# Placing every split weight load 60 places earlier in the scheduling order of a two-layer hybrid decoder trunk

## The chip, the cores and the metric

The kernel is one program on one core of a Trainium2 chip. The metric is the device time of one execution in microseconds (us), as the median of several runs. Beside it stands one execution that was taken with the hardware profiler; its span is the time from the first to the last instruction that the profiler recorded.

## The reference

Two layers act on a sequence of 512 tokens with 1024 features, in 32-bit floats. What one layer computes, cut to what matters here:

```
h = rmsnorm(x, norm_mix_pre)
proj = h @ w_in
q, k, v, rw, gate_a, gate_b = _split(proj, ...)
y_att = sliding_window_attention(rope(q), rope(k), v, att_sinks) @ w_o_att
y_rw = rwkv7_time_mix(rw, ...) @ w_o_rw          # delta-rule state over the tokens
mixed = sigmoid(gate_a) * y_att + sigmoid(gate_b) * y_rw
x = x + rmsnorm(mixed @ w_out, norm_mix_post)
u = causal_dwconv(rmsnorm(x, norm_ffn_pre) @ w_up, conv_w, conv_b)
ua, ub = _split(u, (FFN_DIM, FFN_DIM))           # FFN_DIM = 2816
x = x + rmsnorm((gelu(ua) * ub) @ w_down, norm_ffn_post)
x = x + rmsnorm(sigmoid(x @ w_ple_gate) * (p[i] @ w_ple), norm_ple)
```

## The kernel before

All activations are held with features on the 128 partitions and the 512 tokens along the free axis, so a weight matrix is cut into tiles of 128 x 128 and one output tile is 128 features by 512 tokens. `KT` is 8: a product over 1024 features has 8 such k-tiles, the product over the 2816 features of `w_down` has 22.

**A product in three parts.** Each operand is split into a high part, rounded to the fast matmul format `F32R`, and a low part, the rest. `mm3` (L250 to L252) adds three matmuls for each k-tile: high weight by high activation, high weight by low activation, low weight by high activation.

**A weight load.** `load_w` (L134) brings up to four k-tiles at once, 256 KB: a DMA into `w`, which SyncE issues (L122); on ScalarE the rounding copy into `wh` (L125); on VectorE the difference `w` minus `wh` into `wl` (L155). The buffers come in two classes. Class `m` has two buffers for `w` and three each for `wh` and `wl`, class `f` has one for `w` and two each for the others. Most loops take the classes in turn; inside the attention and state stages most loads are of class `m`. `proj` issues, for each four k-tiles, one load and the twelve matmuls that use it. So a load with its matmuls takes 15 places in program order, a product over eight k-tiles 30 places, one output tile of `w_down` 84.

A second group of helpers, `raw_w`, `split_raw` and `keep_w`, loads weights which are kept for later; their raw DMA target comes from the same `w` buffers when no other pool is named, but the code is not `load_w`.

**The stages of a layer**, in program order: a lead-in that normalizes and computes a few small projections; attention (`w_q`, `w_g`, `w_ga`); four groups of the state stage (`rwkv_group`), in each of which `rwkv_prep` runs twice and projects with `w_k`, `w_wa2`, `w_r` and `w_v`, `rwkv_inverse` makes a triangular inverse of 62 dependent VectorE steps and several small DMAs, and then eight chunks are scanned one after another with small matmuls; the gate `w_gb`; the output products `w_oa` and `w_or`; `w_out`; a small product with `w_ple`, whose results are stored as `ed`; the convolution stage (`ffn`, 44 products with `w_up`, each followed by one rescaling `un`, one ScalarE and two VectorE steps `cv`); `w_down`, with four `keep_w` loads of `w_pg` put between its columns; and the gate `w_pg`.

**What sets the order.** The program is written in one sequence, and each instruction's priority is its place in that sequence. A scheduler of the tile framework then builds the queue of each engine before the program runs: among the instructions that it takes to be ready, the one with the lowest number goes first. The queues are then fixed, and the engines work through them in order, with semaphore waits where an operand or a buffer is not free. A block under `tc.high_priority(offset=n)` gives the instructions in it numbers that are `n` lower. The seams between the stages use an offset of 3000 (`turn`), and `behind` and `issue_after` tie some instructions behind a named one. Before the change, the products of the convolution stage stood under an offset of 40, loads and matmuls together.

## Time and profile before

| what | us |
| --- | --- |
| median of 3 runs | 2319.58 |
| lowest and highest | 2317.64 and 2322.39 |
| the profiled execution | 2329.03 |
| its span | 2327.3 |
| mean granted TensorE clock in it | 0.981 of full speed |

In the profile, TensorE's matmuls stand as PE, its weight loads into the array as PEld, VectorE as DVE, ScalarE as ACT, GpSimd as POOL and SyncE's queue as SP or SPq. A group is a line of the kernel with its engine, operation and tiles; after the bar come busy time, the mean of one instruction in ns, and the idle time of that engine just before, with what ended it. A wait is written as the engine and tile that waited, the work that released it, the total in us, how often, and the longest. A helper's line stands for all its callers, so L125 and L122 are told apart by the tile names. One caution holds throughout: matmuls overlap in the hardware and their ends are modelled, so the mean of one 128x512 matmul in the records is longer than the distance between two starts.

### The profile page before, as it was taken

What the parts mean: (1) busy time and instruction counts of PE and PEld (TensorE: products, weight loads), DVE (VectorE), ACT (ScalarE), POOL (GpSimd) and SP (SyncE); (2) the same over time, 40 slices, a digit from 0 to 9 for tenths busy, and PEclk for the clock granted to TensorE, in tenths of its full rate; (3) what the DMA queues carried; (4) which work ended last, traced back from release to release, by engine and by line L of the source; (5) the groups of instructions that cost most, each with busy time, mean ns of one, the idle gap of its engine ahead of it and who ended that gap; (6) DMA issues with size and microseconds to landing.
All of it is one profiled execution on the core that took longest, in us unless ns stands there. A gap on an engine that the chain in (4) does not pass through costs nothing. (4 is left out here: it accounts for less than half of the span.)

```text
span 2327.3 us, 39473 instructions
## 1 busy us (share of the span) xinstructions
PE 2228.8 (96%) x14340; PEld 1740.2 (75%) x14340; DVE 1546.9 (66%) x3683; ACT 1109.6 (48%) x2450; POOL 27.1 (1%) x86
## 2 busy tenths in 40 slices
PE   7999999999999999999899999998999999999997
PEld 6766776667689777788896677766777887777886
DVE  6764678767566777743877647778656667776346
ACT  5566455544444544432445655545443544444332
POOL 1000000000000000000000000000000000000000
PEclk9999999889999999999999999999999999999998
DMA  4532332245571423233234333333356623223432
GB/s 150 168 94 97 99 94 79 75 121 171 176 259 31 128 91 98 89 118 116 86 124 148 98 104 98 83 92 103 113 159 212 213 78 92 95 95 90 126 98 69
DMA packets 204515, 269.40 MB, mean 116 GB/s; under 512 B 71840, under 2 KB 84640, under 8 KB 204320
## 3 DMA queue, kind: packets, MB, share of 16 engines
q1 hardware_dynamic: 204320, 266.88, 37.3%
q8 instruction: 113, 1.85, 0.3%
q14 instruction: 82, 0.67, 0.1%
HBM read 218.95 MB, written 42.47 MB: 112 GB/s over the span
## 5 line engine op out<-in xcount | busy, mean ns | idle before, releaser
L155 DVE TENSOR_TENSOR wl<-w,wh 128x512 fp32r<-128x512 f32 (+2 forms) x574 | 373.9, 662 | 317.4 <-ACT wh L125 292.7
L125 ACT ACTIVATE wh<-w 128x512 fp32r<-128x512 f32 (+1 forms) x590 | 348.8, 604 | 477.8 <-PE pm L251 134.7
L250 PE MATMUL pm<-hh,wh 128*128 128x512 f32 x1040 | 423.0, 412 | 4.6 <-ACT wh L125 2.4
L252 PE MATMUL pm<-hh,wl 128*128 128x512 f32 x1040 | 417.1, 408 | 7.4 <-DVE wl L155 7.2
L251 PE MATMUL pm<-hl,wh 128*128 128x512 f32 x1040 | 416.3, 404 | 0.0
L250 PEld LDWEIGHTS pm<-hh,wh 128*128 128x128 f32 x1040 | 196.8, 189 | 63.3 <-ACT wh L125 11.2
L252 PEld LDWEIGHTS pm<-hh,wl 128*128 128x128 f32 x1040 | 196.9, 189 | 57.5 <-DVE wl L155 13.6
L251 PEld LDWEIGHTS pm<-hl,wh 128*128 128x128 f32 x1040 | 197.4, 190 | 44.1 <-issue 7.2
L250 PE MATMUL pf<-hh,wh 128*128 128x512 f32 x512 | 208.3, 407 | 9.5 <-ACT hh L125 3.6
L251 PE MATMUL pf<-hl,wh 128*128 128x512 f32 x512 | 203.7, 398 | 0.0
L252 PE MATMUL pf<-hh,wl 128*128 128x512 f32 x512 | 203.5, 398 | 0.1
L134 DVE SCALAR_TENSOR_TENSOR cv<-un,vec,cv 128x511 f32<-128x511 f32 (+1 forms) x176 | 130.5, 749 | 40.6 <-ACT cv L125 38.1
L250 PEld LDWEIGHTS pf<-hh,wh 128*128 128x128 f32 x512 | 96.2, 188 | 42.7 <-ACT wh L125 8.5
L252 PEld LDWEIGHTS pf<-hh,wl 128*128 128x128 f32 x512 | 96.6, 189 | 27.0 <-issue 4.4
L251 PEld LDWEIGHTS pf<-hl,wh 128*128 128x128 f32 x512 | 96.7, 189 | 19.6 <-issue 1.8
L125 ACT ACTIVATE cv<-un,vec 128x512 f32<-128x512 f32 x88 | 71.1, 814 | 66.7 <-DVE un L128 66.7
L250 PE MATMUL pm<-uh,wh 128*128 128x512 f32 (+1 forms) x248 | 89.2, 360 | 3.5 <-ACT wh L125 3.4
L252 PE MATMUL pm<-uh,wl 128*128 128x512 f32 (+1 forms) x248 | 89.3, 360 | 0.0
L251 PE MATMUL pm<-ul,wh 128*128 128x512 f32 (+1 forms) x248 | 88.9, 359 | 0.0
L128 DVE TENSOR_TENSOR acc<-acc,sq 128x256 f32<-128x256 f32 (+1 forms) x114 | 50.0, 463 | 31.2 <-ACT sq L125 30.5
L533 DVE CUSTOM_DVE_ANT_0 sm<-scores,tmask 128x256 f32<-128x256 f32 (+1 forms) x128 | 43.5, 385 | 37.3 <-PE scores L117 37.1
L697 DVE TENSOR_TENSOR Z<-rin,Z 128x126 f32<-128x126 f32 (+22 forms) x248 | 62.3, 251 | 4.3
(409 smaller groups left out, 4468.9 us busy)
## 6 DMA issues: line engine op xcount, KB each, us to landing
w<-in_w_up_dram SPq DMA_DIRECT2D x156, 256.0 KB
w<-in_w_dn_dram SPq DMA_DIRECT2D x80, 256.0 KB
w<-in_w_q_dram SPq DMA_DIRECT2D x32, 256.0 KB
w<-in_w_ga_dram SPq DMA_DIRECT2D x32, 256.0 KB
w<-in_w_k_dram SPq DMA_DIRECT2D x32, 256.0 KB
w<-in_w_r_dram SPq DMA_DIRECT2D x32, 256.0 KB
w<-in_w_v_dram SPq DMA_DIRECT2D x32, 256.0 KB
w<-in_w_gb_dram SPq DMA_DIRECT2D x32, 256.0 KB
```

The costliest lines, as they stand in the source:

```text
L125: return self.nc.scalar.activation(out=out, in_=in_, func=func, **kw)
L128: return self.nc.vector.tensor_tensor(out=out, in0=in0, in1=in1, op=op)
L134: return self.nc.vector.scalar_tensor_tensor(out=out, in0=in0, scalar=s, in1=in1, op0=op0, op1=op1)
L155: self.nc.vector.tensor_tensor(out=wl, in0=w, in1=wh.bitcast(F32), op=ALU.subtract)
L250: mm(ps, wh, ah, start=start, stop=False)
L251: mm(ps, wh, al, start=False, stop=False)
L252: return mm(ps, wl, ah, start=False, stop=stop).ins
L533: nc.vector.tensor_tensor_reduce(out=sm[i][:, par * 256:par * 256 + KW], in0=scs[par][:, x * 256:x * 256 + KW], in1=tm, scale=1.0, scalar= ...
L697: nc.vector.tensor_tensor(out=tv, in0=rin[:, jj:jj + 1, jj + 1:].broadcast_to([P, n, nt]), in1=zt[:, :n, jj:jj + 1].broadcast_to([P, n, nt ...
```

## The change

`load_w` keeps the choice of the buffer class and then puts everything else, the DMA, `wh`, the optional partial corrections (L148) and `wl`, under an offset of 60. The body moves to a new method without another edit. In the convolution stage, the block with the offset of 40 goes away: its matmuls return to their own places, and its loads go from 40 to 60 places ahead.

```diff
@@ -139,6 +139,10 @@
             self.nw = (self.nw + 1) % 2
             cls = "mf"[self.nw]
         nb = {"m": (2, 3, 3), "f": (1, 2, 2)}[cls]
+        with self.tc.high_priority(offset=60):
+            return self.load_parts(src, kn, width, cls, nb, low)
+
+    def load_parts(self, src, kn, width, cls, nb, low):
         w = self.wpool.tile([P, kn, width], F32, name="w", tag="w" + cls, bufs=nb[0])
         self.dma(w, src)
         wh = self.wpool.tile([P, kn, width], F32R, name="wh", tag="wh" + cls, bufs=nb[1])
@@ -1098,8 +1102,7 @@
                 for k, w in enumerate(ahead[m]):
                     self.mm3(ps, w, h[k], k == 0, k == KT - 1)
             else:
-                with self.tc.high_priority(offset=40):
-                    ps = self.proj(a["w_up"][l, m], h, key=m)
+                ps = self.proj(a["w_up"][l, m], h, key=m)
             t, s = Y("cv"), F("un")
             self.tt(s, ps, self.rs, ALU.mult)
             self.act(t, s, AF.Identity, scale=vv("cw2")[:, m:m + 1], bias=vv("cb")[:, m:m + 1])
```

No instruction, transfer or buffer is added or removed. The loads that `raw_w` and `keep_w` make keep their places.

## The prediction

> **What bounds the kernel now.** I read the page first, then the stretches of 50 us, then TensorE's own waits.

> ```profile
> span 2327.3 us, 39473 instructions
> PE 2228.8 (96%) x14340; PEld 1740.2 (75%) x14340; DVE 1546.9 (66%) x3683; ACT 1109.6 (48%) x2450; POOL 27.1 (1%) x86
> L155 DVE TENSOR_TENSOR wl<-w,wh 128x512 fp32r<-128x512 f32 (+2 forms) x574 | 373.9, 662 | 317.4 <-ACT wh L125 292.7
> L125 ACT ACTIVATE wh<-w 128x512 fp32r<-128x512 f32 (+1 forms) x590 | 348.8, 604 | 477.8 <-PE pm L251 134.7
> ```

> TensorE is busy 2228.8 of 2327.3 us, so all its idle time together is 98.5 us. The change can take away idle time of TensorE and nothing else: the two split operations cost 662 and 604 ns before and after, 574 and 590 times. The idle time is spread unevenly.

> ```profile
> 350.00:400.00 50.00, 44.66 (x405) 29.28 (x404) 46.28 (x131) 29.05 (x69) 1.75 (x5) 0.98 0.31 87
> 400.00:450.00 50.00, 49.64 (x569) 33.81 (x569) 29.52 (x85) 24.62 (x70) 0.00 (x0) 0.78 0.26 76
> 850.00:900.00 50.00, 50.00 (x216) 39.57 (x215) 36.40 (x55) 23.01 (x36) 0.00 (x0) 1.00 0.29 95
> ```

> The columns are the stretch, its length, then busy time of PE, PEld, DVE, ACT and POOL, the granted clock, the DMA share and GB/s. In the convolution stage (850 to 900) TensorE has no idle time at all. In the state stage (350 to 400) it is idle for 5.34 us and VectorE is busy for 46.28 of 50. The list of TensorE's waits names what ends them:

> ```profile
> PE lead L250 <- ACT kwh L125: 15.3, 1, 15.3
> PE rstd L290 <- DVE nry L134: 8.3, 6, 6.5
> PE pm L252 <- DVE wl L155: 8.0, 10, 1.7
> PE pm L250 <- ACT wh L125: 7.4, 8, 1.9
> PE pm L250 <- ACT yr L125: 5.8, 4, 2.2
> PE A L117 <- DVE AR L128: 5.3, 3, 2.4
> PE half L250 <- ACT tg L125: 5.0, 1, 5.0
> PE pf L250 <- ACT hh L125: 3.6, 2, 2.4
> PE pm L600 <- ACT thw L125: 2.9, 2, 2.0
> PE A L117 <- DVE AM L128: 2.7, 4, 1.9
> PE pf L250 <- ACT wh L125: 2.5, 5, 0.8
> PE ple L250 <- ACT wh L125: 2.1, 2, 1.0
> PE pf L252 <- DVE wl L155: 0.4, 1, 0.4
> ```

> The first row is the start of the kernel, loaded through `raw_w`, which the change doesn't touch. The rows that end in `wh` or `wl` are those a load can cause: 8.0 + 0.4 for `wl` and 7.4 + 2.5 + 2.1 for `wh`, **20.4 us in all**, 0.9% of the span. The rest waits for other results.

> **The change part by part.** *Work.* Nothing is added or removed, so every engine's own sum is the same, zero us. Each load moves with its DMA issue on SyncE, its `wh` on ScalarE and its `wl` on VectorE, 60 places, which is two products of 30 places. How far it can really move is set by the buffers: class `m` holds three `wh`, class `f` two, so at most five loads, two and a half products, can stand ahead of the matmuls. The page's row of `wh` shows 134.7 us of ScalarE idle until a matmul (L251) gives a `wh` buffer back. Those loads are already as early as their buffers let them be, and a smaller number moves none of them. So only the others count.

> *The waits for wl, 8.4 us.* One of the longest, with the VectorE rows before it:

> ```profile
> 387.75 0.68 DVE L128 TENSOR_TENSOR Di<-k,Di 128x512 f32<-128x512 f32 x1
> 388.35 0.19 DVE L699 TENSOR_TENSOR Z<-Z 128x45 f32<-128x45 f32 x1
> 388.47 0.68 DVE L155 TENSOR_TENSOR wl<-w,wh 128x512 fp32r<-128x512 f32 x1
> 389.20 0.50 PE L252 MATMUL pm<-hh,wl 128*128 128x512 f32 x1 [1.37 <-DVE wl L155]
> ```

> `wl` stands in a busy queue behind steps of the same preparation (`Di`) and of the inverse (`Z`), and TensorE waits 1.37 us for it. `Di` stands less than 60 places ahead of the products it overlaps, so the new number lets `wl` pass it; one place earlier in the queue is worth 0.68 us here, two cover the whole wait. Bounds: 0 and 8.4 us. I take all **8.4**, because the cause here is queue order on VectorE, just what the change acts on.

> *The waits for wh, 12.0 us.* Here the transfer is late. An example, in SyncE's and ScalarE's queues:

> ```profile
> 394.08 0.33 SPq L122 DMA_DIRECT2D yrd<-yo  x1
> 394.45 0.92 SPq L122 DMA_DIRECT2D w<-in_w_v_dram  x2
> 398.14 0.63 ACT L125 ACTIVATE wh<-w 128x512 fp32r<-128x512 f32 x1 [2.54 <-DMA w<-in_w_v_dram]
> 397.26 1.16 PE L117 MATMUL A<-AR,bk 64*128 64x128 f32 x16 [2.38 <-DVE AR L128]
> ```

> The two `w_v` loads are issued right behind a store of the group before; the first lands for 398.14. A load whose issue passes such a store gains what the store holds up. TensorE's 2.38 us before the `A` matmuls is put down to `AR`, but with `w_v` in place it would have had other matmuls to run. A further case is the small `w_ple` product, whose loads share SyncE with the `ed` stores, and the columns of `w_down`. There, the chain that ended last runs through the one buffer of class `f`:

> ```profile
> 2158.50 2.65 DMA w<-in_w_pg_dram
> 2161.17 0.64 ACT kwh L125
> 2161.83 0.70 DVE kwl L128
> 2162.55 2.71 DMA w<-in_w_dn_dram
> ```

> A `w_pg` load of `keep_w`, which keeps its place, holds that buffer from 2158.50 to 2162.55, 4.05 us. The `w_down` loads, 60 places earlier, may now pass it. But a landing that is late because its buffer was late stays late. Bounds: 0 and 12.0; nothing tells the two kinds apart row by row, so I take half, **6.0**.

> *What is pushed back.* Each load that moves forward puts something else back by one `wl` or `wh`, 0.66 or 0.60 us. This costs only where TensorE already waits for such a result: `yr` 4 times, `AR` 3, `hh` 2, `thw` 2, `AM` 4, 15 waits in the rows above. With 0.66 us each that is 9.9 us; the other end is nothing. `AR`, `AM` and `thw` stand in the preparation, where the loads are passed over them, so 9 of the 15, **6.0 us**, is my value.

> *The matmuls of the convolution stage* lose their 40 places. In that stage TensorE's queue holds no other work than these products, and the row at 850 shows it full, so their order among themselves stays; 0. At its front the products of `w_ple` come first again, by program order; each matmul has to be run once in either order. If that cover failed, the stage would show idle time that it doesn't have now. Its loads go from 40 to 60 places, bounded by the same five buffers; 0. A later `un` can hold back an accumulator, but three accumulators give it two further products to finish in; 0.

> *The sum*: 8.4 + 6.0 - 6.0 = 8.4 us off the profiled span, 2327.3 to 2318.9. The profiled execution took 2329.03, of which 1.7 lie outside the span, and stands 9.45 above the median. I take the same 8.4 off the median: 2319.58 - 8.4 = **2311.2 us**, 0.36% faster.

> *The clock.* The stretch from 400 to 450 has the clock at 0.78, with TensorE busy for 49.64 us of it, many of them tiny matmuls. 22% of 50 us, 11 us, is the most that a better filled stretch there could give; it stays out of the sum, because I can't tell whether the loads would fill it. [...]

> **The rivals.**

> *Buffers, not places: no change.* The 134.7 us above, 105 times, is ScalarE waiting for TensorE. If the 20.4 us are likewise set by buffers and landings, gains and push-backs cancel: 2319.6, with 3 us to either side. Against it stands the `wl` case, which is a matter of places in one queue.

> *A load parks in front of the scan: slower.* ScalarE and VectorE work through fixed queues. A `wh` that was put ahead of a scan step's copy (`scr`, `X`, `Y`), because the scheduler took its transfer as landed, stalls that copy until the transfer has really landed. The place is the `w_k` load that opens each preparation while the group before is scanned:

> ```profile
> ACT wh L125 <- DMA w<-in_w_k_dram: 35.2, 10, 7.4
> PE xs L778 <- ACT scr L125: 2.0, 4, 0.8
> ```

> ScalarE already waits 35.2 us there in 10 waits, at no cost now, as the scan's own wait for `scr` is just 2.0 us. If each of the ten came ahead of a scan step and TensorE had nothing else, the price would be 35.2 us: 2354.8. With other products covering half, 17.6 us: 2337.2. It decides as soon as more than 8.4 of these 35.2 us fall on the scan. For it: 60 places reach back over the 39 closing steps of a group and into its last chunk, which has 34. Against it: the other seven chunks are out of reach. [...]

> *More than the sum*: all 20.4 us, the 5.3 us of `AR` and the 11 us of clock, 36.7 us in all: 2282.9.

> *The change does nothing it says* is excluded only in part: the numbers do change, but a queue that is already in this order stays so. It is the first rival's case.

> **How the numbers follow.** The forecast, 4.6 to 15 us faster, 0.48; more than that, 0.08; no change, 0.23; slower, 0.21. About 0.2%, 4.6 us, is what a measurement of this kernel can tell from no change. So faster 0.56, same 0.23, slower 0.21. The range goes from 2288, where nothing is pushed back and the clock is won as well (2319.6 - 20.4 - 11 = 2288.2), to 2335, just under the half price of the slower rival; each side leaves out about one in ten. Gains alone: 2304 to 2315.

> **What would show it.** Right: the two `wl` rows among TensorE's waits fall from 8.4 to under 3 us, the three `wh` rows from 12.0 to about 6, the `AR`, `AM` and `thw` rows grow by up to 6 us, and TensorE's idle sum falls from 98.5 to about 90. The convolution stretches stay at 50.00. Wrong, to the slow side: new rows of TensorE waiting on `scr`, `X` or `Y`, or idle time in the convolution stage; the clock in the state stage under 0.9 in more stretches than now. Wrong, to the other: state stage and `w_down` shorter by more than their waits.

## The result and the profile after

| | before | after |
| --- | --- | --- |
| median us (4 runs each) | 2319.93 | 2280.27 |
| lowest and highest | 2317.64, 2322.39 | 2275.79, 2284.78 |
| span of the profiled execution | 2327.3 | 2274.1 |
| mean granted clock in it | 0.981 | 0.993 |

The ratio is 0.9825, with a 95% interval from 0.9807 to 0.9843: **39.7 us faster**. The forecast was 8.4 us, and the time lies below its range. Of the four runs after, three list a mean clock of 0.990 to 0.993 and one, of 2284.78 us, lists 0.942; no trace of that run is kept, so this figure stays unexplained.

The page of the kernel after, and its stretches of 50 us beside those quoted of before (stretch, length, busy PE, PEld, DVE, ACT and POOL with the count of instructions, granted clock, DMA share, GB/s):

```profile
span 2274.1 us, 39486 instructions
PE 2192.8 (96%) x14340; PEld 1730.1 (76%) x14340; DVE 1544.7 (68%) x3683; ACT 1120.0 (49%) x2450; POOL 26.7 (1%) x86
```

```profile
350.00:400.00 50.00, 48.74 (x440) 33.47 (x435) 47.21 (x134) 29.05 (x71) 1.75 (x5) 1.00 0.32 90
400.00:450.00 50.00, 47.87 (x618) 32.36 (x618) 37.75 (x102) 29.62 (x82) 0.53 (x1) 1.00 0.31 86
850.00:900.00 50.00, 50.00 (x222) 41.42 (x221) 37.85 (x55) 24.61 (x37) 0.00 (x0) 1.00 0.32 95
```

TensorE's own busy time fell by 36.0 us, from 2228.8 to 2192.8, with the same 14340 matmuls; its idle time fell only from 98.5 to 81.3. So most of the gain lies where TensorE counted as busy. Two columns show it. From 400 to 450 the clock went from 0.78 to 1.00. From 850 to 900, where busy was 50.00 and still is, the *count* went from 216 to 222.

The waits that the prediction worked with, in the kernel after:

```profile
PE pm L254 <- ACT wh L125: 6.0, 9, 1.3
PE A L117 <- DVE AM L128: 4.1, 9, 1.8
PE pm L604 <- ACT thw L125: 3.7, 4, 1.8
PE pm L256 <- DVE wl L159: 2.9, 5, 0.9
PE A L117 <- DVE AR L128: 1.2, 1, 1.2
PE pf L254 <- ACT wh L125: 0.6, 2, 0.3
```

The rows that end in `wl` or `wh` went from 20.4 to 9.5 us.

Two parts of the program hold most of the gain. The first two rows are the state stage's scans of each layer, from their first small matmul (`xs`) to the first product of `w_or`; the last two are the convolution stage of each layer, from the last `w_ple` matmul to the first of `w_down`. Before:

```profile
337.10:625.30 288.20, 277.53 (x2685) 196.13 (x2682) 205.59 (x561) 141.98 (x355) 4.73 (x14) 0.93 0.40 117
1492.10:1773.40 281.30, 268.88 (x2684) 191.35 (x2683) 206.69 (x561) 142.07 (x354) 4.73 (x14) 0.97 0.41 121
766.50:987.40 220.90, 218.72 (x938) 173.21 (x937) 165.02 (x246) 105.54 (x164) 0.00 (x0) 1.00 0.31 96
1912.60:2134.20 221.60, 220.41 (x939) 170.53 (x938) 165.40 (x246) 104.72 (x163) 0.00 (x0) 1.00 0.31 97
```

After:

```profile
337.70:605.20 267.50, 261.82 (x2683) 183.62 (x2682) 202.54 (x559) 140.83 (x353) 4.72 (x14) 1.00 0.42 125
1458.30:1730.00 271.70, 262.45 (x2684) 183.91 (x2682) 203.66 (x559) 140.48 (x354) 4.72 (x14) 1.00 0.42 123
745.30:959.70 214.40, 212.99 (x938) 175.63 (x937) 169.56 (x250) 112.53 (x169) 0.00 (x0) 1.00 0.33 101
1869.00:2083.40 214.40, 212.93 (x938) 175.65 (x937) 169.16 (x250) 112.50 (x168) 0.00 (x0) 1.00 0.34 102
```

The scans take 569.5 us before and 539.2 after, 30.3 less; the convolution stages 442.5 and 428.8, 13.7 less; the rest of the 53.2 us between these two spans is 9.2.

Multiply length by mean clock in the scan rows: 268.0 and 272.9 before, 267.5 and 271.7 after. The clock has two digits, so each product is good to about 1.4 us; within that, both kernels need the same time at full clock. **Nearly the whole gain in the scans is clock**: before, 7% and 3% of the two stretches, 20.2 and 8.4 us, were lost to half clock. This is an account of the time, not yet a cause: TensorE's idle time in the same rows fell too, from 23.1 to 14.9 us. Where one such spell of before begins and ends (windows of a few us, same columns):

```profile
390.00:397.00 7.00, 4.80 (x20) 3.30 (x18) 6.19 (x14) 1.75 (x3) 1.22 (x4) 1.00 0.64 156
397.00:400.00 3.00, 2.33 (x20) 1.52 (x20) 2.41 (x5) 1.26 (x2) 0.00 (x0) 0.73 0.72 150
400.00:421.00 21.00, 21.00 (x201) 15.07 (x200) 5.13 (x13) 3.59 (x12) 0.00 (x0) 0.50 0.24 59
421.00:425.00 4.00, 4.00 (x55) 2.75 (x55) 2.26 (x6) 1.88 (x6) 0.00 (x0) 0.84 0.11 36
```

It begins just behind the 2.38 us wait before the `A` matmuls that the prediction quoted, and holds for 21 us in which TensorE is "busy" for all 21.00. In the kernel after, that wait is gone. VectorE's rows (other work between them left out) and one of SyncE's show why:

```profile
378.36 0.69 DVE L128 TENSOR_TENSOR AM<-A,amask 128x512 f32<-128x512 f32 x1
379.30 0.68 DVE L159 TENSOR_TENSOR wl<-w,wh 128x512 fp32r<-128x512 f32 x1
379.98 0.25 DVE L701 TENSOR_TENSOR Z<-rin,Z 128x91 f32<-128x91 f32 x1
380.23 0.68 DVE L159 TENSOR_TENSOR wl<-w,wh 128x512 fp32r<-128x512 f32 x1
380.01 1.27 SPq L122 DMA_DIRECT2D w<-in_w_v_dram  x2
```

Two `wl` of that preparation are now done at 379 to 381, among the `Z` steps of the inverse and ahead of its `Di`. Before, the first of them ran at 388.47, behind `Di`. In `load_w`, `wl` is the last step that reads `w`, so it gives the buffer back for a further transfer. The two `w_v` transfers now go out from 380.01 on, when the first `wl` has just ended (379.98), and not from 394.45 on as before. So the `w_v` matmuls are there for TensorE to run while it would have waited for `AR`.

### The profile page after: what moved, and what is told of

It reads as the page before. It is cut to its first block, busy times and chain, and to the rows that moved or that the text cites. A ratio compares the mean times of both kernels' runs of the same rounds, so it can differ in the third digit from the quotient of the medians.

```text
span 2274.1 us, 39486 instructions
## 1 busy us (share of the span) xinstructions
PE 2192.8 (96%) x14340; PEld 1730.1 (76%) x14340; DVE 1544.7 (68%) x3683; ACT 1120.0 (49%) x2450; POOL 26.7 (1%) x86
## 5 line engine op out<-in xcount | busy, mean ns | idle before, releaser
L125 ACT ACTIVATE wh<-w 128x512 fp32r<-128x512 f32 (+1 forms) x590 | 352.9, 605 | 514.5 <-PE pm L255 173.3
L255 PE MATMUL pm<-hl,wh 128*128 128x512 f32 x1040 | 415.3, 399 | 0.0
L255 PEld LDWEIGHTS pm<-hl,wh 128*128 128x128 f32 x1040 | 195.3, 188 | 41.5 <-issue 2.4
L255 PE MATMUL pf<-hl,wh 128*128 128x512 f32 x512 | 203.2, 397 | 0.5 <-DVE hl L128 0.5
L134 DVE SCALAR_TENSOR_TENSOR cv<-un,vec,cv 128x510 f32<-128x510 f32 (+1 forms) x176 | 130.8, 749 | 23.2 <-ACT cv L125 20.6
L255 PEld LDWEIGHTS pf<-hl,wh 128*128 128x128 f32 x512 | 96.7, 189 | 21.0 <-DVE hl L128 1.2
L255 PE MATMUL pm<-ul,wh 128*128 128x512 f32 (+1 forms) x248 | 88.9, 359 | 0.0
L125 ACT ACTIVATE cv<-un,vec 128x512 f32<-128x512 f32 x88 | 71.2, 814 | 28.3 <-DVE un L128 28.2
L128 DVE TENSOR_TENSOR acc<-acc,sq 128x256 f32<-128x256 f32 (+1 forms) x114 | 49.9, 462 | 38.5 <-ACT sq L125 38.0
L128 DVE TENSOR_TENSOR un<-pm,rs 128x512 f32<-128x512 f32 x56 | 38.5, 690 | 39.8 <-PE pm L256 39.8
L703 DVE TENSOR_TENSOR Z<-Z 128x126 f32<-128x126 f32 (+22 forms) x248 | 62.0, 250 | 3.7
```

The lines of the kernel that those rows point to most:

```text
L125: return self.nc.scalar.activation(out=out, in_=in_, func=func, **kw)
L128: return self.nc.vector.tensor_tensor(out=out, in0=in0, in1=in1, op=op)
L134: return self.nc.vector.scalar_tensor_tensor(out=out, in0=in0, scalar=s, in1=in1, op0=op0, op1=op1)
L255: mm(ps, wh, al, start=False, stop=False)
L703: nc.vector.tensor_tensor(out=zt[:, :n, jj + 1:], in0=zt[:, :n, jj + 1:], in1=tv, op=ALU.add)
```

## The experiments

### Which stage: the state stage alone, all but the state stage, all but the convolution stage

In this part each ratio is against the kernel before, measured again beside the experiment; its medians were 2321.16 to 2325.85 us.

A field, `ahead_by`, gives the offset by stage. The cut shows it for the loads of the state stage alone, against the kernel before. The second kernel has 0 and 60 exchanged and the convolution stage as after; the third has 60 all over but in the convolution stage, which keeps its old 40.

```diff
+        self.ahead_by = 0
...
+        with self.tc.high_priority(offset=self.ahead_by):
+            return self.load_parts(src, kn, width, cls, nb, low)
...
+            self.ahead_by = 60
             R = self.rwkv(l, rp)
+            self.ahead_by = 0
```

The state stage alone:

> Loads 60 places ahead in the state stage alone; every other load and the convolution stage as before. Theory C (in the state stage the queue order decides how much of the time the TensorE clock stands at half; at full clock its two scan stretches take 267 to 273 us a layer in every kernel so far): the scans lose most of the 58 us at half clock, about 25 to 30 us faster than before, 2290 to 2296, the convolution stage stays near 220. Rival D (the half clock is chance of the execution and the gain comes from the borders of the other stages): no more than 10 us faster, 2310 or above.

Measured: 2291.52 us, ratio 0.9863 (0.9847 to 0.9880).

All but the state stage:

> As the changed kernel, but loads in the state stage stand at their own places. Theory C: keeps the convolution stage and the borders, loses the clock: 2298 to 2306, with 40 us or more at half clock in the state stage. Rival D: about 2285.

Measured: 2305.16 us, ratio 0.9923 (0.9905 to 0.9942).

All but the convolution stage:

> Loads 60 places ahead in all stages except the convolution stage, which keeps its 40 for loads and matmuls together. Theory A: the convolution stage stays at 220 us per layer and the kernel gains 20 to 28 us, in the state stage and at the stage borders, so 2292 to 2300. Rival B: about 2280 less the few us of the borders, nearly the whole gain, or if the convolution stage was the whole effect, no gain.

Measured: 2280.85 us, ratio 0.9830 (0.9808 to 0.9851).

The scan rows of the first two kernels, two layers each, with the state stage's loads moved:

```profile
337.70:611.70 274.00, 263.22 (x2684) 186.29 (x2683) 204.44 (x561) 141.76 (x355) 4.72 (x14) 0.98 0.42 124
1472.70:1742.70 270.00, 261.95 (x2685) 183.69 (x2683) 204.04 (x560) 141.03 (x354) 4.72 (x14) 1.00 0.43 124
```

and with all others moved:

```profile
340.40:627.00 286.60, 274.27 (x2683) 194.49 (x2683) 206.91 (x561) 142.41 (x354) 4.72 (x14) 0.94 0.40 119
1480.70:1761.80 281.10, 268.95 (x2685) 191.41 (x2683) 206.39 (x561) 142.05 (x354) 4.72 (x14) 0.96 0.41 121
```

The loads of the state stage decide whether the clock falls there; theory C holds, D falls. The two gains, 32 and 19 us against the 2323.70 of before measured beside them, add up to more than the 40 of both: the parts share something. The third kernel shows what, and the first agrees. Their convolution stages keep the old offset and take 217.1 and 215.4 us in the third, 217.8 and 214.7 in the first, not the 220 that was expected of both. So 10.0 of that stage's 13.7 us came without touching its own priorities; an earlier change of the queues carries on into it. The third kernel as a whole is as fast as the full change within the intervals, where theory A had 2292 to 2300: the change in the convolution stage adds nothing clear to the rest.

### The convolution stage: its offset removed, and the change in that stage alone

First, the kernel before without the two lines of the offset:

```diff
-                with self.tc.high_priority(offset=40):
-                    ps = self.proj(a["w_up"][l, m], h, key=m)
+                ps = self.proj(a["w_up"][l, m], h, key=m)
```

> The kernel before without the offset of 40 in the convolution stage; no load is moved anywhere. Theory A (the matmuls of the convolution stage alternated between two accumulators and lost about 0.1 us at each array load that waited; their own places end that): about 15 us faster than before, 2305, with 936 matmuls of the stage in about 213 us instead of 220 and 221. Rival B (the loads being 60 places ahead is what fills the convolution stage): no faster than before, or slower, since the loads there lose 40 places.

Measured: 2314.76 us (one of the ten runs took 8400.32; the median of the others is 2314.34), ratio 0.9971 (0.9950 to 0.9992), the stage at 220.0 and 217.8 us, not 213. But from 850 to 900 it ran 223 matmuls to the 216 of before, at the same 50.00 busy:

```profile
850.00:900.00 50.00, 50.00 (x223) 41.39 (x222) 38.77 (x57) 25.33 (x38) 0.00 (x0) 1.00 0.30 98
773.74 0.80 PE L252 MATMUL pm<-hh,wl 128*128 128x512 f32 x1 [3.54 <-DVE wl L155]
773.70:780.50 6.80, 6.76 (x18) 5.33 (x19) 4.98 (x8) 1.73 (x3) 0.00 (x0) 0.56 0.42 121
```

The last two rows take it back: at the start of the stage TensorE waits 3.54 us for a `wl`, and runs the next 6.8 us at a mean clock of 0.56. So the matmuls at their own places make the stage dense, and the loads ahead are needed for its start. Both together, in that stage alone, by the same field as above:

> The change in the convolution stage alone: its loads 60 places ahead, its matmuls at their own places, all other loads as before. Its queue order in that stage has few alternations between the accumulators. Theory A: 213 to 215 us a layer in that stage instead of 220.9 and 221.6, so 12 to 15 us faster than before, about 2307, with the state stage's half clock unchanged. If the state stage alone carries the gain: within 5 us of before.

Measured: 2308.81 us, ratio 0.9923 (0.9887 to 0.9958), the stage at 214.8 and 213.4 us. Theory A is right about the size of this stage and half right about the cause. What the matmuls lost before can be seen where the accumulator changes (`pm` to `pf`, in the kernel before):

```profile
934.00 0.39 PE L250 MATMUL pm<-hh,wh 128*128 128x512 f32 x1
934.27 0.50 PE L250 MATMUL pf<-hh,wh 128*128 128x512 f32 x1
934.60 0.40 PE L251 MATMUL pf<-hl,wh 128*128 128x512 f32 x1
934.84 0.40 PE L252 MATMUL pf<-hh,wl 128*128 128x512 f32 x1
```

Starts stand 0.23 us apart, but 0.33 us after the first `pf`. The overlap of the records hides 0.1 us: the next matmul starts late, and busy has no hole. From 800 to 960 us, the starts that come over 0.03 us later than a distance of 0.227 us add up to some 4 us in before and to nothing from 780 to 940 in the kernel after. The array loads of before wait for `un` at such places, 27 times in the first layer's stage; with the change, once:

```profile
PEld pm L250 <- DVE un L128: 5.0, 18, 0.3
PEld pf L250 <- DVE un L128: 2.5, 9, 0.3
```

```profile
PEld pm L254 <- DVE un L128: 0.2, 1, 0.2
```

In the second layer of before, array loads also wait 34 times for `wh` and 16 times for `wl`. With all but the convolution stage changed, these waits are gone there, but for one, and in each layer some 18 short ones are left, put down to `un` or to nothing that the profile shows. So much is seen of how the earlier change carries on into this stage.

### Which part of a load

The transfer alone 60 places ahead, then only the rounding copy with the difference, then only one of these (the offset then stands around its one line); the convolution stage's matmuls are at their own places in all four.

```diff
-        with self.tc.high_priority(offset=60):
-            return self.load_parts(src, kn, width, cls, nb, low)
...
+        with self.tc.high_priority(offset=DMA_AHEAD):
+            self.dma(w, src)
+        with self.tc.high_priority(offset=SPLIT_AHEAD):
+            return self.split_parts(src, kn, width, cls, nb, low, w)
```

The transfer alone:

> As the changed kernel, but only the transfer of each load stands 60 places ahead; rounding copy and difference stand at their own places. Theory A1 (queue order on ScalarE and VectorE is what made the split parts late): keeps the convolution stage's 15 us and loses most of the rest, about 2300. Theory A2 (the issue on SyncE behind stores was what made loads late): about 2282.

Measured: 2309.10 us, ratio 0.9956 (0.9938 to 0.9974).

Copy and difference:

> As the changed kernel, but only the rounding copy and the difference stand 60 places ahead; the transfer is issued at its own place. Theory A1: about 2282, the whole gain. Theory A2: about 2300.

Measured: 2279.63 us, ratio 0.9829 (0.9808 to 0.9849).

The difference alone:

> As the changed kernel, but only the difference on VectorE stands 60 places ahead; transfer and rounding copy stand at their own places. Theory G (VectorE's queue, as the prediction argued): about 2282, with 20 us or less at half clock in the two state stages. Rival H (ScalarE's queue): about 2305, half clock of 50 us or more.

Measured: 2292.77 us, ratio 0.9859 (0.9820 to 0.9898).

The copy alone:

> As the changed kernel, but only the rounding copy on ScalarE stands 60 places ahead. Theory G: about 2305, half clock of 50 us or more in the two state stages. Rival H: about 2282. If both are needed, both kernels come out between 2290 and 2305.

Measured: 2315.20 us, ratio 0.9944 (0.9919 to 0.9968).

VectorE's queue is what matters, as theories A1 and G have it, though G's 2282 was missed by 11 us. The intervals of the transfer alone and of the copy alone overlap with that of the convolution stage's matmuls at their own places (0.9971), which both contain, so neither shows a gain of its own. Whether ScalarE's copy adds to the difference is not clear either: 0.9829 and 0.9859 overlap. The scan rows of the first layer say the same by their clock, for the transfer alone and for the difference alone:

```profile
338.20:626.90 288.70, 277.34 (x2686) 197.25 (x2682) 206.76 (x561) 142.39 (x354) 4.72 (x14) 0.93 0.39 119
```

```profile
339.80:615.10 275.30, 268.28 (x2683) 189.35 (x2682) 202.74 (x559) 141.59 (x354) 4.73 (x14) 0.97 0.41 122
```

The buffer tells why. The first `wl` of the preparation and the `w_v` transfers, with the transfer alone ahead, then with the difference alone:

```profile
389.61 0.69 DVE L165 TENSOR_TENSOR wl<-w,wh 128x512 fp32r<-128x512 f32 x1
395.60 0.92 SPq L123 DMA_DIRECT2D w<-in_w_v_dram  x2
```

```profile
381.38 0.68 DVE L160 TENSOR_TENSOR wl<-w,wh 128x512 fp32r<-128x512 f32 x1
382.09 1.27 SPq L122 DMA_DIRECT2D w<-in_w_v_dram  x2
```

A transfer with a number 60 lower still goes out behind `wl`, which has to give its buffer back, and behind the same stores as before. With `wl` early, the transfer goes out 12 us earlier than before's 394.45 although its own number is unchanged, 0.03 us after that `wl` has ended (382.06). TensorE's 2.38 us wait for `AR` is still there in the first kernel and gone in the second.

### How far ahead

`offset=60` becomes 30, then 120.

> As the changed kernel with 30 places, one product, for 60. If the gain comes from loads being early in general, about 2280 to 2288, with at most a few us at half clock in the state stage. If the 60 hit upon a lucky order (rival E), anywhere between 2280 and 2320, with half clock coming back.

Measured: 2294.09 us, ratio 0.9876 (0.9854 to 0.9899).

> As the changed kernel with 120 places, four products, for 60. If the gain comes from loads being early, and at most five loads fit the buffers, about 2280, as with 60. Rival E: anywhere between 2280 and 2320. If loads can be too early, so that they stand in front of the scan, slower than 2285 with new waits of the scan steps.

Measured: 2289.37 us, ratio 0.9854 (0.9839 to 0.9868).

Both are faster than before, so loads that are early help in general. Neither reaches 60 (the interval of 120 just touches its 0.9807 to 0.9843), so part of its last 10 us is a matter of the order that came out. With 30 places the time lies outside the 2280 to 2288 of the first reading, and half clock came back, as rival E had it: both scans have a mean clock of 0.96. With 120 they stand at 1.00 and 0.99, and the loss is elsewhere: the convolution stages take 218.6 and 219.3 us. The slower kernel with new waits of the scan, which the third reading of `off120` and the prediction's rival had in view, didn't come.

### The same queues once more

Both kernels unedited, one more profile each.

> The kernel before once more, the same queues. [...]

Measured: 2321.37 us, the scans 284.4 and 283.1 us at a clock of 0.95 and 0.96.

> The changed kernel once more, the same queues. Theory C: again little half clock in the state stage, under 15 us in both layers together, and a span within 8 us of 2274. Rival D (chance): 30 us of half clock or more.

Measured: 2278.30 us, the scans 267.6 and 274.0 us at 1.00 and 0.99.

With the same queues the half clock comes out differently from one execution to the next, but the two kernels stay apart. The first profile of before took 9 us more than the median; against this second pair the 43.1 us between the spans (2319.7 and 2276.6) are 25.9 us in the scans and 13.9 in the convolution stages, with 3.3 elsewhere. That is the account nearest to the medians. Length by mean clock, over all kernels of this study except the one with pauses:

| kernel | first layer | second layer |
| --- | --- | --- |
| before, twice | 268.0, 270.2 | 272.9, 271.8 |
| after, twice | 267.5, 267.6 | 271.7, 271.3 |
| state stage alone; all but it | 268.5; 269.4 | 270.0; 269.9 |
| all but the convolution stage | 267.3 | 272.3 |
| convolution stage alone; without offset | 270.3; 268.6 | 272.0; 270.4 |
| transfer; copy and difference | 268.5; 267.6 | 269.2; 271.4 |
| difference; copy | 267.0; 270.6 | 271.7; 272.9 |
| 30 places; 120 places | 265.9; 268.5 | 266.7; 268.5 |

The lengths themselves go from 267.3 to 293.9 us; at full clock all lie between 265.9 and 272.9.

### Pauses in a dense stream

To see what a wait costs by itself, six pauses were put into each convolution stage of the kernel after.

```diff
+        def pause(ps, n):
+            with tc.high_priority(offset=PRIO):
+                z = self.small.tile([P, P], F32, name="pz", bufs=1)
+                self.act(z, ps[:, 0:P])
+                for _ in range(n - 1):
+                    self.act(z, z)
+                pp = self.PT("pause")
+                self.hold = self.nc.tensor.matmul(pp[:, 0:1], z[:, 0:P], self.ones1, start=True, stop=True).ins
...
+                with tc.issue_after(self.hold) if self.hold else ExitStack():
+                    ps = self.proj(a["w_up"][l, m], h, key=m)
```

> The changed kernel, with six pauses put into TensorE's dense stream in each layer's convolution stage, 33 us apart: a chain of 2, 4, 6, 8, 11 and 15 ScalarE copies (the second layer in reverse order) and a one-column matmul behind it, which the next products wait for. By about 0.25 us a copy they should last from 0.8 to 4 us. Theory C (a wait of some 2 us is enough to bring the clock to half about 11 us later): half clock of 3.4 us or more after the pauses of 2 us and longer, none after the shortest two. [...]

The 11 us in the expectation were a misreading. In windows of 0.2 us the half clock has begun at most 0.6 us after the end of a pause of 2.93 us or more, and 1.4 us after the end of the one pause of 1.68 us that it followed. Measured: one run of 2343.37 us. The pauses lasted 1.0 to 6.5 us. One of 2.93 us, with some of the rows around it, and one of 1.46 us:

```profile
845.47 0.39 PE L256 MATMUL pm<-hh,wl 128*128 128x512 f32 x1
848.78 0.38 PE L1108 MATMUL pause<-ones,pz 128*128 128x1 f32 x2 [2.93 <-ACT pz L125]
849.38 0.63 PE L255 MATMUL pm<-hl,wh 128*128 128x512 f32 x1
849.80 0.63 PE L256 MATMUL pm<-hh,wl 128*128 128x512 f32 x1
852.75 0.39 PE L254 MATMUL pm<-hh,wh 128*128 128x512 f32 x1
777.80 0.38 PE L1108 MATMUL pause<-ones,pz 128*128 128x1 f32 x2 [1.46 <-ACT pz L125]
778.36 0.40 PE L255 MATMUL pm<-hl,wh 128*128 128x512 f32 x1
```

```profile
848.70:852.60 3.90, 3.81 (x11) 3.06 (x12) 2.75 (x4) 0.66 (x2) 0.00 (x0) 0.58 0.09 33
```

After the 2.93 us a matmul lasts 0.63 us for 3.4 us, then 0.39 again. Half clock followed all eight pauses of 2.93 us and more, one of the two of 1.68 us, and neither of the shortest two (1.46 and 1.0 us), as theory C had it. The spells behind these pauses are 3.4 us or 6.8 us, and those in the scans of before 23.9, 3.4 and 13.6 us in the first layer and 3.4, 3.4 and 10.2 us in the second, near whole multiples of 3.4.

What this doesn't show is why the clock also falls in the scans without a wait. The spell of 13.6 us in the kernel before, with the 10 us ahead of it, in which no wait of TensorE is recorded:

```profile
484.00:494.00 10.00, 9.96 (x107) 8.00 (x107) 5.74 (x10) 3.34 (x7) 0.00 (x0) 1.00 0.32 73
494.00:507.60 13.60, 13.60 (x150) 10.12 (x146) 6.16 (x15) 4.21 (x13) 0.00 (x0) 0.50 0.22 56
```

The one of 10.2 us is like it (no wait in the 8 us before), so 23.8 of the 58 us at half clock there belong to spells that begin without a wait. Many matmuls in front of these spells are tiny, 32*32 by 32x32: 64 of the 107 from 484 to 494 us, and 128 of the 165 from 1634 to 1644. What brings the clock down there is not shown.

## Why the prediction was wrong

*Only idle time can be won.* This first step failed. It read "busy 50.00 of 50" as a full engine. 36.0 of the 53.2 us between the profiled spans came out of busy time.

*The convolution stage, 0.* It failed by 13.7 us. The cover that was named, a queue with no idle time, was there and hid nothing: 216 matmuls to the stretch were the sign, against the 222 that the same window holds in the kernel after. The array loads' waits for `un`, 7.5 us in the first layer, were not read, only those of the matmuls. The stage alone, changed, gave 214.8 and 213.4 us.

*The clock, left out of the sum.* It failed by most of the scans' 25.9 to 30.3 us, the largest error. The bound of 11 us was taken from one stretch of 50 us only; 20.2 us were lost to half clock in the first layer's scans and 8.4 in the second's. The doubt whether the loads would fill that stretch should have carried a term of its own.

*The waits for wl, 8.4 us.* Right in kind: they fell by 5.5, to 2.9, and the difference alone, in VectorE's queue, gives most of the gain. The size of what hangs on it, the clock, was missed.

*The waits for wh, 6.0 of 12.0 us.* Right in size, taken as a half without a measurement: 12.0 fell to 6.6 (6.0 + 0.6, and no row for `ple` is left). The reason was only partly right. That TensorE would have other matmuls to run with `w_v` in place came true, but what put the `w_v` transfers behind the stores was the late `wl`, which kept their buffer, and not their own number: moved alone, they stayed there, and the scans' clock stayed at 0.93 and 0.94. For `w_ple` the reason fits: with the transfer alone its products take 13.9 us in place of 15.2 from the first start to the last, in each layer.

*What is pushed back, 6.0 us.* Wrong in sign. `AR`, `AM` and `thw` went from 10.9 to 9.0 us: `AM` and `thw` did grow, by 2.2 together, but `AR` fell by 4.1, since the matmuls of `w_v` filled a wait of 2.38 us.

*The rivals.* Buffers, not places: no, although `wh` still waits for buffers (173.3 us of ScalarE idle until L255, 134.7 before), and buffers set when a transfer starts, by way of the place of `wl`. The parked load: no sign of it; TensorE's wait for `scr` is 1.7 us. "More than the sum", 2282.9, lies 2.6 us from the result, with the right kind of cause, the clock, and without the convolution stage. That it comes so near is luck: of its 20.4 us of waits 10.9 were won and of its 5.3 of `AR` 4.1, while its 11 us of clock were too few by more than half.

## What to carry over

Count instructions per stretch beside the busy share: matmuls that overlap can lose a tenth of a microsecond each (here 0.33 us from start to start for 0.23) without a hole in the busy time. Multiply the length of a stretch by its mean clock before looking for causes; if two orders agree at full clock, the difference is clock, and a wait can stand ahead of a loss several times its size (here 2.38 us ahead of a spell of 23.9 us at half clock, some 12 us lost). Ask which step gives a buffer back: here the cheap part of a load, a 0.66 us difference in a crowded queue, decided when the next transfer could start, and moving it alone, with the convolution stage's matmuls at their own places, gave 33 us.
